# Softmax denominators taken off the output matmuls and summed elementwise, in a two-layer attention and convolution kernel

## The chip, the cores and the metric

One core of a Trainium2 chip (trn2). The metric is device time of one execution in microseconds; of several runs the median counts. Engines are named as in the profile: PE is TensorE (PEld its weight loads), DVE is VectorE, ACT ScalarE, POOL GpSimd, SP SyncE, which here only issues DMAs.

## What is computed

A backbone of two layers over 1024 latent tokens (width 1024) with a prefix of 256 context tokens, in float32. Layer 0 has two groups of heads: global attention over all 1280 tokens (A) and banded attention of 128-query blocks over the context and at most three neighbouring 128-key blocks (B), whose context queries also have a learned sink logit in the denominator. Layer 1 has a convolution branch and a 2-D neighbourhood attention with a bias table (D). Every attention is

```python
s = jnp.einsum("bqhgd,bkhd->bhgqk", q, k) * ATTN_SCALE + bias
p = jax.nn.softmax(s, axis=-1)
o = jnp.einsum("bhgqk,bkhd->bqhgd", p, v)
```

followed by a SiLU gate, an output projection, and a residual scaled by a modulation vector, `silu(c) @ mod_w + mod_b`. A last RMSNorm gives the result.

## The kernel before, in words

To keep float32 accuracy, matmul operands are split in two: `split` (L329) makes a high part on ACT (L331) and subtracts it from the source on POOL or DVE for the low part (L334). A product is then three matmuls, high·high, low·high and high·low; `mm3` (L352 to L354) does it for the projections.

**Attention** is one generator, `attn_gen` (L463), for both layers. Its work is a list of groups, and a group is a list of key tiles. In layer 0 a group is one 128-query block of one unit (`group0`, L621; four heads side by side, 512 columns). Units 2 and 3 are B, units 0 and 1 are A, in the order 2, 3, 0, 1. A B group has two context tiles and, for latent blocks (`qb >= 2`), two or three band tiles: 4 or 5 tiles, with 8 such groups in a unit. A context group has 2 tiles, and a latent A group 10. In layer 1 a group is one half of the grid of one head (`group1`, L1355): 7 tiles, of 512, 256, 352, 512, 320, 224 and 512 columns; there are 16 groups.

For a tile, PE forms the scores in bank `st` (L529, L533), ACT takes the exponential into `pf` (L541; in layer 1 DVE adds the bias first, L538), ACT makes `ph` and POOL, or every 12th (layer 0) or 5th (layer 1) time DVE, makes `pl`. Three tiles later `flush` (L470) adds the tile to the group's output bank `ov`, which has one buffer. The value tile is 192 wide: low part of V, high part of V, and 64 columns of ones. So three matmuls of the tile's columns,

```python
PE.matmul(o, V[:, 64:192], ph[:, :n], start=(t == 0), stop=False)
PE.matmul(g.ov[0:64, q0 : q0 + n], V[:, 0:64], ph[:, :n], start=False, stop=False)
PE.matmul(o, V[:, 64:192], pl[:, :n], start=False, stop=(last and g.sink is None))
```

(L480, L481, L482) give the output in rows 0 to 63 and the denominator, 64 times, in rows 64 to 127. After the last tile DVE transposes the denominators (L490), takes the reciprocal (L492), spreads it again (L493), and `finish` (L689 in layer 0, L1426 in layer 1) multiplies it onto the output (L693, L1430) and applies the gate (L695, L1432).

**Order.** `weave` (L562) advances the attention generator and a generator of other work by turns: in layer 0 the projections of the next unit, in layer 1 the projections `d_proj` of the last heads and the output projections `out1`. While units 2 and 3 are made, `tick` also advances `mod_steps` (L215), which computes eight 512-wide halves of the modulation vectors. For a half it loads two `mw` tiles of 1024 KB (L221) one half ahead, and multiplies each by four blocks of `csil` (`mod_part`, L181, matmuls at L185). Bank `tr` has one buffer too; layer 0 uses it for transposes of keys and queries (`trk`, L932). A scheduler then puts each engine's instructions in an order of its own, by priorities; on the chip every engine takes them strictly in that order, SP's DMA issues included.

Of the kernel before, what the change touches and what calls it, by code (L numbers as in the profile page):

```python
# [10 lines left out]
F32 = mybir.dt.float32  # L11
# [22 lines left out]
LOOK0, LOOK1 = 3, 3  # L34
AHEAD = 3
# [54 lines left out]
def tile_kernel(ctx: ExitStack, tc: tile.TileContext, a, out):  # L90
# [11 lines left out]
    mk, mwp, layer = [0], [None], [0]  # L102
# [112 lines left out]
    def mod_steps(pool, halves):  # L215

        def load(l, part, j):
            ws = []
            for d in (0, 4):
                w = pool.tile([P, 4, 512], F32, tag="mw", name=nm("mw"), bufs=2)  # L220
                SY.dma_start(w, mod_src(l, part, j, d, d + 4))  # L221
                ws.append(w)
            return ws

        ws = load(*halves[0])
        for n_, hf in enumerate(halves):
# [4 lines left out]
            for d, w in enumerate(ws):  # L231
                mod_part(pb, w, range(4 * d, 4 * d + 4))
# [5 lines left out]
            if n_ + 1 < len(halves):  # L238
                ws = load(*halves[n_ + 1])
# [156 lines left out]
    def v_tiles(pool, n, bufs=1):  # L396
        Vs[:] = [pool.tile([P, n, 192], F32R, tag="V", name=nm("Vt"), bufs=bufs) for _ in range(bufs)]
        for V in Vs:
            GP.memset(V[:, :, 128:192].bitcast(F32), 1.0)
# [63 lines left out]
    def attn_gen(pool, groups, vshare, look, nexts=None):  # L463
# [6 lines left out]
        def flush():  # L470
# [9 lines left out]
            PE.matmul(o, V[:, 64:192], ph[:, :n], start=(t == 0), stop=False)  # L480
            PE.matmul(g.ov[0:64, q0 : q0 + n], V[:, 0:64], ph[:, :n], start=False, stop=False)  # L481
            PE.matmul(o, V[:, 64:192], pl[:, :n], start=False, stop=(last and g.sink is None))  # L482
            if last:
                if g.sink is not None:
                    PE.matmul(g.ov, g.skm(), g.QL[0:76, :], start=False, stop=True)
                r1 = pool.tile([P, 8, 32], F32, tag="r1", name=nm("r1"), bufs=1)
                r8 = pool.tile([P, 8], F32, tag="r8", name=nm("r8"), bufs=2)
                rb = pool.tile([P, 256], F32, tag="rb", name=nm("rb"), bufs=1)
                for e in range(2):
                    VE.transpose(r1[e * 64 : (e + 1) * 64].rearrange("p a b -> p (a b)")  # L490
                                 .rearrange("p (a q) -> p a q", a=2), g.den(g.ov[64:128, :], e))
                VE.reciprocal(r8, r1[:, :, 0])  # L492
                VE.transpose(rb, r8[:, :, None].broadcast_to([P, 8, 32]))  # L493
                g.finish(g.ov, rb)
# [23 lines left out]
        for x, (g, t) in enumerate(items):  # L518
# [17 lines left out]
            pf = pool.tile([P, 512], F32, tag="pf" if layer[0] else "ost", name=nm("pf"), bufs=PFB)  # L536
# [7 lines left out]
            pend.append((g, t, ph, pl))  # L544
            if t == len(g.tiles) // 2:
                g.gate()
# [73 lines left out]

    def group0(u, qb):  # L621
# [64 lines left out]
        def den(dn, e):  # L686
            return dn.rearrange("p (e f q) -> p f e q", f=2, e=2)[:, :, e, :]

        def finish(ov, rb):  # L689
            y = a0.tile([P, 2, P], F32, tag="y", name=nm("y"), bufs=YB)  # L690
            for e in range(2):
                es = slice(e * 64, (e + 1) * 64)
                VE.tensor_tensor(y[es], den(ov[0:64, :], e), rb[es, :].rearrange("p (a q) -> p a q", a=2),  # L693
                                 op=ALU.mult)
# [4 lines left out]
            else:  # L699
# [7 lines left out]
                  tiles=[(k, 0, 512, x) for k, x in kt], den=den, finish=finish)  # L707
# [276 lines left out]
    with tc.tile_pool(name="o0", bufs=1, reuse_waits="tile") as op_:  # L984
# [49 lines left out]
        def final_proj(c):  # L1034
# [3 lines left out]
            pool, tag, bufs = (kvp, "QH", 3) if c == 2 else (op_, "acc1", 1)  # L1038
# [5 lines left out]
            for e in range(DK):  # L1044
# [15 lines left out]
                else:  # L1060
                    if c < 2:
                        sq = op_.tile([P, 512], F32, tag="sq1", name=nm("sq1"), bufs=3)
                    else:
                        sq = kvp.tile([P, 512], F32, tag="QL", name=nm("sq1"), bufs=3)
# [670 lines left out]
```

## Time and profile before

| | |
|---|---|
| three runs | 1527.92, 1532.71, 1538.26 us; median 1532.71 |
| the profiled execution | span 1528.5 us; the page gives no other time for it |
| busy share | PE 95%, PEld 76%, DVE 67%, POOL 52%, ACT 49% |
| layer 0's B units | about 120 to 500 us; A units to about 905 us |
| between the attentions | about 905 to 1170 us, projections and convolution |
| layer 1's attention | about 1200 to 1505 us |

Times in a trace count from the span's start. A row of a group gives line, engine, operation, tiles and shapes, how often it ran, its busy time and the mean of one in ns, and behind the bar the idle time of the engine just before. PE's busy time counts a matmul from start to modelled end, and neighbours overlap; what one costs in a stream is the distance from start to start.

### The profile page before, as it was taken

To read this page: it belongs to the slowest core of one execution; us is meant where nothing else is said; L and a number is where in the kernel's file an instruction comes from. 1 tells how busy PE (TensorE), PEld (TensorE's weight loads), DVE (VectorE), ACT (ScalarE), POOL (GpSimd) and SP (SyncE) were. 2 spreads that over 40 slices of the span, in tenths; PEclk is the share of its full clock that TensorE was granted. 3 is DMA by queue.
4 is the path that set the end of the run, shared out by engine and by line. 5 is a ranking of instruction groups with operands and counts; after the bars stand their busy time and mean duration, and the time that the engine had idled before them with its cause. 6 is when DMAs were issued, how large, how long until landed. Compare 5 with 4: busy or idle time off the path is not lost.

```text
span 1528.5 us, 21545 instructions
## 1 busy us (share of the span) xinstructions
PE 1451.0 (95%) x7144; PEld 1167.2 (76%) x7144; DVE 1031.7 (67%) x2095; ACT 748.1 (49%) x1418; POOL 788.0 (52%) x628
## 2 busy tenths in 40 slices
PE   6999999998998999999999889999999999989996
PEld 2786877896896777886777568888887788868775
DVE  2643566589578856457676948899848666567766
ACT  3642433443435564447646665343334455455564
POOL 3360443555454766557645665665532434364665
PEclk9999999999999999999999999999999999989998
DMA  9564325422312246121202021210484677877642
GB/s 366 201 225 135 106 69 174 135 77 88 114 56 76 85 138 210 49 69 54 59 28 66 35 67 56 62 56 28 158 253 144 207 219 240 248 222 234 178 129 110
DMA packets 154167, 199.83 MB, mean 131 GB/s; under 512 B 14716, under 2 KB 95816, under 8 KB 154056
## 3 DMA queue, kind: packets, MB, share of 16 engines
q1 hardware_dynamic: 147392, 186.88, 38.9%
q10 hardware_dynamic: 6664, 11.57, 2.3%
q8 instruction: 56, 0.92, 0.3%
q14 instruction: 55, 0.45, 0.1%
HBM read 148.07 MB, written 49.02 MB: 129 GB/s over the span
## 4 chain that ended last, share of the span: by engine, by line
PE 79%; DVE 11%; issue 3%; DMA 3%; ACT 2%; POOL 1%; ACTq 0%; SPq 0%; DVEq 0%; POOLq 0%
PE p L352 6%; PE p L354 6%; PE p L353 6%; PE ov L480 5%; PE ov L482 4%; PE ov L481 4%; PE po L352 4%; PE st L533 4%; PE st L529 4%; PE po L353 4%; PE po L354 4%; PE pq L352 4%; PE pq L353 3%; PE pq L354 3%; PE pg L352 2%
## 5 line engine op out<-in xcount | busy, mean ns | idle before, releaser
L334 POOL TENSOR_TENSOR pl<-pf,ph 128x512 fp32r<-128x512 f32 (+4 forms) x321 | 394.0, 1239 | 384.9 <-ACT ph L331 337.3
L541 ACT ACTIVATE pf<-st 128x512 f32<-128x512 f32 x284 | 166.5, 597 | 203.6 <-PE st L533 165.2
L334 POOL TENSOR_TENSOR wl<-wr,wh 128x512 fp32r<-128x512 f32 (+2 forms) x131 | 169.3, 1302 | 136.5 <-ACT wh L331 124.0
L331 ACT CAST ph<-pf 128x512 fp32r<-128x512 f32 (+4 forms) x364 | 209.5, 588 | 27.1 <-PE ov L481 15.9
L352 PE MATMUL p<-hh,wh 128*128 128x512 f32 x448 | 176.0, 393 | 3.4 <-DVE spq L1233 1.3
L353 PE MATMUL p<-hl,wh 128*128 128x512 f32 x448 | 174.5, 390 | 0.0
L354 PE MATMUL p<-hh,wl 128*128 128x512 f32 x448 | 173.0, 391 | 0.0
L480 PE MATMUL ov<-ph,Vt 128*128 128x512 f32 (+4 forms) x364 | 141.0, 387 | 4.2 <-DVE y L693 2.0
L529 PE MATMUL st<-QH,KAt 128*128 128x512 f32 (+4 forms) x364 | 140.2, 386 | 3.9 <-ACT pf L541 3.1
L482 PE MATMUL ov<-pl,Vt 128*128 128x512 f32 (+4 forms) x364 | 141.1, 388 | 2.2 <-POOL pl L334 2.1
L481 PE MATMUL ov<-ph,Vt 128*64 128x512 f32 (+4 forms) x364 | 138.9, 381 | 0.0
L533 PE MATMUL st<-QL,KBt 68*128 68x512 f32 (+4 forms) x364 | 136.4, 386 | 0.9 <-issue 0.8
L1177 DVE SCALAR_TENSOR_TENSOR cps<-U,taps,cps 128x512 f32<-128x512 f32 x184 | 125.9, 748 | 0.7
L331 ACT CAST wh<-wr 128x512 fp32r<-128x512 f32 (+2 forms) x134 | 80.9, 613 | 84.1 <-PE po L353 15.9
L352 PEld LDWEIGHTS p<-hh,wh 128*128 128x128 f32 x448 | 84.2, 188 | 21.5 <-ACT spq L1231 1.6
L656 DVE TENSOR_REDUCE mp<-mx 128x1 f32<-128x512 f32 x128 | 85.3, 681 | 19.3 <-PE mx L655 18.3
L354 PEld LDWEIGHTS p<-hh,wl 128*128 128x128 f32 x448 | 84.1, 188 | 17.4
L353 PEld LDWEIGHTS p<-hl,wh 128*128 128x128 f32 x448 | 84.2, 188 | 17.1 <-issue 0.2
L1020 DVE SCALAR_TENSOR_TENSOR x<-po,modT,x 128x512 f32<-128x512 f32 (+1 forms) x72 | 46.9, 657 | 64.0 <-PE po L354 63.5
L352 PE MATMUL pq<-wh,hh 128*128 128x384 f32 x256 | 88.2, 344 | 1.0 <-ACT hh L331 1.0
L353 PE MATMUL pq<-wl,hh 128*128 128x384 f32 x256 | 87.3, 341 | 0.0
L354 PE MATMUL pq<-wh,hl 128*128 128x384 f32 x256 | 86.6, 342 | 0.0
(287 smaller groups left out, 3417.2 us busy)
## 6 DMA issues: line engine op xcount, KB each, us to landing
mw<-in_mod_w_dram SPq DMA_DIRECT2D x16, 1024.0 KB, 5.3
Q<-qs SPq DMA_DIRECT2D x40, 256.0 KB, 2.1
QH<-Q SPq DMA_DIRECT2D x80, 128.0 KB, 2.7
mw<-in_mod_w_dram SPq DMA_DIRECT2D x16, 512.0 KB, 6.8
wr<-in_od_d_dram SPq DMA_DIRECT2D x32, 256.0 KB, 3.1
wr<-in_ev_qkv_dram SPq DMA_DIRECT2D x16, 384.0 KB, 5.0
KAt<-KD SPq DMA_DIRECT2D x16, 384.0 KB, 6.5
wr<-in_od_wo_dram SPq DMA_DIRECT2D x22, 256.0 KB, 3.4
```

What stands on the lines that cost most here:

```text
L331: acts.append(SC.copy(hi, src))
L334: (GP if leng == "g" else VE).tensor_tensor(lo, src, hi.bitcast(F32), op=ALU.subtract)
L352: PE.matmul(o, lh, rh, start=first, stop=False)
L353: PE.matmul(o, lh, rl, start=False, stop=False)
L354: last.append(PE.matmul(o, ll, rh, start=False, stop=end))
L480: PE.matmul(o, V[:, 64:192], ph[:, :n], start=(t == 0), stop=False)
L481: PE.matmul(g.ov[0:64, q0 : q0 + n], V[:, 0:64], ph[:, :n], start=False, stop=False)
L482: PE.matmul(o, V[:, 64:192], pl[:, :n], start=False, stop=(last and g.sink is None))
L529: sts.append(PE.matmul(st[:, :n], KA[:, cs], g.QH[:, q0 : q0 + n], start=True, stop=False))
L533: PE.matmul(st[:, :n], KB[0:68, cs], g.QL[0:68, q0 : q0 + n], start=False, stop=True)
L541: acts.append(SC.activation(pf[:, :n], st[:, :n], AF.Exp, scale=1.0 if g.bias else SCALE))
L1177: VE.scalar_tensor_tensor(pc, uc, w, pc, op0=ALU.mult, op1=ALU.add)
```

## The change

Where a group has `adds` set (latent groups of units 2 and 3, 16 in all, and all 16 groups of layer 1), the ones no longer go through the matmul of every tile:

- the exponentials of the group's first tile are written to an accumulator `acc`, and each later tile's `pf` is added to it, on POOL or, for every fourth tile (`t = 4` in layer 0, `t = 2` and `t = 6` in layer 1), on DVE;
- per tile PE does two matmuls instead of three: both halves of V by `ph` at once, with the low part of V into rows 0 to 63 of `ov` and the high part into rows 64 to 127, and the high part by `pl` into rows 0 to 63. The low·high product therefore waits in the other half of the bank;
- at the end of the group `acc` is split into two parts (ACT and DVE) and multiplied by 64 columns of ones, two matmuls of 512 columns into a bank `dn` of tag `tr`, and the sink follows;
- `finish` first copies rows 64 to 127 of `ov` to SBUF on ACT and adds rows 0 to 63 on DVE, which frees `ov`, and then transposes, inverts and multiplies. In layer 1 both transposes run over 64 x 512 instead of 64 x 256 twice and 128 x 256.

Other groups do as before. `mod_steps` loads tiles of 512 KB, three buffers instead of two of 1024 KB, and issues the load of chunk n+3 after the matmuls of chunk n. Layer 1's value tile is 128 wide, and its fill with ones is gone. Between the layers some scratch tiles change their pool.

```diff
+ADV = (0, 2)
+UADD = (2, 3)
...
-        ws = load(*halves[0])
+        ws = []
+        for n in range(3):
+            load(n)
...
-            for d, w in enumerate(ws):
-                mod_part(pb, w, range(4 * d, 4 * d + 4))
+            for d in range(4):
+                mod_part(pb, ws.pop(0), (2 * d, 2 * d + 1))
+                if 4 * n_ + d + 3 < 4 * len(halves):
+                    load(4 * n_ + d + 3)
...
-            PE.matmul(o, V[:, 64:192], ph[:, :n], start=(t == 0), stop=False)
-            PE.matmul(g.ov[0:64, q0 : q0 + n], V[:, 0:64], ph[:, :n], start=False, stop=False)
-            PE.matmul(o, V[:, 64:192], pl[:, :n], start=False, stop=(last and g.sink is None))
-            if last:
+            if g.adds:
+                both = [(o, V[:, 0:128], ph), (o[0:64], V[:, 64:128], pl)]
+                for x_, v_, p_ in both[::-1] if last else both:
+                    PE.matmul(x_, v_, p_[:, :n], start=(t == 0 and p_ is ph), stop=(last and p_ is ph))
...
+            if g.adds:
+                dn = bank("tr", nm("dn"))
+                for k_, x in enumerate(g.acs):
+                    PE.matmul(dn[0:64, :], ones64[0] if layer[0] else V[:, 128:192], x, start=(k_ == 0), stop=(k_ == 1 and g.sink is None))
...
+            if g.adds and t == 0:
+                pf = g.acc = pool.tile([P, 512], F32, tag="acc", name=nm("acc"), bufs=2)
...
+            if g.adds and t > 0:
+                a_ = g.acc[:, q0 : q0 + n]
+                (VE if (t + ADV[layer[0]]) % 4 == 0 else GP).tensor_tensor(a_, a_, pf[:, :n], op=ALU.add)
+            if g.adds and t == len(g.tiles) - 1:
+                g.acs = [pool.tile([P, 512], F32R, tag=x, name=nm("ac" + x), bufs=look + 1) for x in ("ph", "pl")]
+                split(g.acc, *g.acs, "s", "v")
...
+    def ADDS(u, qb):
+        return qb >= 2 and u in UADD
...
+                acts.append(SC.copy(y[ds], ov[64:128, :]))
+                VE.tensor_tensor(y[ds], ov[0:64, :], y[ds], op=ALU.add)
+                VE.transpose(r1[ds].rearrange("p a b -> p (a b)"), dn[0:64, :])
+                VE.reciprocal(r8[ds], r1[ds, :, 0])
+                rb = dlow.tile([P, 512], F32, tag="r1", name=nm("rb"), bufs=1)
+                VE.transpose(rb[ds], r8[ds, :, None].broadcast_to([64, 16, 32]))
+                VE.tensor_tensor(y[ds], y[ds], rb[ds], op=ALU.mult)
```

How the scheduler places it, at three places. First PE at the end of layer 1's last group (`ov` the output, `trs` the column sums of the last norm). Before:

```order
L480 MATMUL ov_15325<-ph_15360,Vt_11676 128x320
L481 MATMUL ov_15325<-ph_15360,Vt_11676 64x320
L482 MATMUL ov_15325<-pl_15361,Vt_11676 128x320
L480 MATMUL ov_15325<-ph_15414,Vt_11676 128x224
L481 MATMUL ov_15325<-ph_15414,Vt_11676 64x224
L267 MATMUL trs_15571<-ones,sq_3731_15355 128x2
L482 MATMUL ov_15325<-pl_15415,Vt_11676 128x224
L480 MATMUL ov_15325<-ph_15467,Vt_11676 128x512
L481 MATMUL ov_15325<-ph_15467,Vt_11676 64x512
L267 MATMUL trs_15571<-ones,sq_3737_15384 128x2
```

Here `trs` fills the wait for the last `pl`. With the change:

```order
L483 MATMUL ov_15594<-ph_15628,Vt_11854 128x320
L483 MATMUL ov_15594<-pl_15629,Vt_11854 64x320
L483 MATMUL ov_15594<-ph_15682,Vt_11854 128x224
L483 MATMUL ov_15594<-pl_15683,Vt_11854 64x224
L483 MATMUL ov_15594<-pl_15736,Vt_11854 64x512
L483 MATMUL ov_15594<-ph_15735,Vt_11854 128x512
L493 MATMUL dn_15823<-acph_15742,one_11839 64x512
L493 MATMUL dn_15823<-acpl_15743,one_11839 64x512
L269 MATMUL trs_15843<-ones,sq_3840_15623 128x2
```

Two rows a tile instead of three, and `trs` now stands behind both `dn`.

Second, PE at the seventh half of the modulation (`pm` its bank, `mw` its weights), in the B units. Before, eight blocks from two tiles that were loaded a half earlier:

```order
L185 MATMUL pm_3143<-mw_2212,csil 32x512 x4
L185 MATMUL pm_3143<-mw_2214,csil 32x512
L353 MATMUL pq_3092<-wl_3075,hc_171 128x384
L354 MATMUL pq_3092<-wh_3074,hc_171 128x384
L352 MATMUL pq_3092<-wh_3074,hc_171 128x384
```

With the change:

```order
L187 MATMUL pm_3248<-mw_2076,csil 32x512 x2
L187 MATMUL pm_3248<-mw_2080,csil 32x512 x2
L187 MATMUL pm_3248<-mw_2084,csil 32x512 x2
L535 MATMUL st_3270<-QH_2902,KAt_489 128x512
L681 MATMUL mx_2950<-KAt_489,QH_2902 128x384
L483 MATMUL ov_3267<-pl_3006,Vt_490 64x512
L483 MATMUL ov_3267<-ph_3024,Vt_490 128x512
L483 MATMUL ov_3267<-pl_3025,Vt_490 64x512
L483 MATMUL ov_3267<-ph_3141,Vt_490 128x512
L187 MATMUL pm_3248<-mw_3251,csil 32x512 x2
```

The fourth chunk (`mw_3251`) is loaded into the buffer that the first one (`mw_2076`) leaves, so its DMA starts only after the first row here, and eight other matmul rows stand between.

Third, DVE in layer 1 at the end of a group (`yo` the output). Before:

```order
L490 STREAM_TRANSPOSE r_3468_14450<-ov_14289 64x256 x2
L538 TENSOR_TENSOR pf_14442<-st_14437,bs_14348 128x352
L436 TENSOR_REDUCE nmt_14313<-mp_14252 128x4
L492 RECIPROCAL r_3469_14451<-r_3468_14450 128x8
L493 STREAM_TRANSPOSE rb_14452<-r_3469_14451 128x256
L538 TENSOR_TENSOR pf_14477<-st_14472,bs_14368 128x512
L1430 TENSOR_TENSOR yo<-ov_14289,rb_14452 64x256 x2
```

With the change:

```order
L1463 STREAM_TRANSPOSE r_3625_14902<-dn_14899 64x512
L1462 TENSOR_TENSOR yo<-ov_14729,yo 64x512
L1535 SCALAR_TENSOR_TENSOR x_3329_13914<-po_3683_15083,modT_103,xs_15079 128x256
L1535 SCALAR_TENSOR_TENSOR x_3331_13916<-po_3683_15083,modT_103,xs_15079 128x256
L1464 RECIPROCAL r_3626_14903<-r_3625_14902 64x16
L547 TENSOR_TENSOR pf_14968<-st_14963,bs_14840 128x320
L1447 ISA mx_3614_14863,mp_14853<-mx_3614_14863,bm_14823 128x440
```

`ov` is now read by one DVE row early on, and the wider reciprocal chain follows without it.

More of the change, by code (lines that the diff above doesn't have):

```diff
@@ L101, in tile_kernel @@
     turn = [0, 0]
-    mk, mwp, layer = [0], [None], [0]
+    mk, mwp, layer, ones64 = [0], [None], [0], []
     sts = []
@@ L215, in mod_steps, with load @@
     def mod_steps(pool, halves):
[L217 to L223, printed above, removed]
-        ws = load(*halves[0])
+        def load(n):
+            l, part, j = halves[n // 4]
+            w = pool.tile([P, 2, 512], F32, tag="mw", name=nm("mw"), bufs=3)
+            SY.dma_start(w, mod_src(l, part, j, 2 * (n % 4), 2 * (n % 4) + 2))
+            ws.append(w)
+        ws = []
+        for n in range(3):
+            load(n)
         for n_, hf in enumerate(halves):
@@ L396, in v_tiles @@
     def v_tiles(pool, n, bufs=1):
[L397 to L399 removed]
+        Vs[:] = [pool.tile([P, n, P], F32R, tag="V", name=nm("Vt"), bufs=bufs) for _ in range(bufs)]
     def k_tiles(pool, hi, n, bufs=1):
@@ L479, in flush @@
             o = g.ov[:, q0 : q0 + n]
-            PE.matmul(o, V[:, 64:192], ph[:, :n], start=(t == 0), stop=False)
-            PE.matmul(g.ov[0:64, q0 : q0 + n], V[:, 0:64], ph[:, :n], start=False, stop=False)
-            PE.matmul(o, V[:, 64:192], pl[:, :n], start=False, stop=(last and g.sink is None))
-            if last:
-                if g.sink is not None:
[L485 to L494, printed above, removed]
+            if g.adds:
+                both = [(o, V[:, 0:128], ph), (o[0:64], V[:, 64:128], pl)]
+                for x_, v_, p_ in both[::-1] if last else both:
+                    PE.matmul(x_, v_, p_[:, :n], start=(t == 0 and p_ is ph), stop=(last and p_ is ph))
+            else:
+                PE.matmul(o, V[:, 64:192], ph[:, :n], start=(t == 0), stop=False)
+                PE.matmul(o[0:64], V[:, 0:64], ph[:, :n], start=False, stop=False)
+                PE.matmul(o, V[:, 64:192], pl[:, :n], start=False, stop=(last and g.sink is None))
+            if not last:
+                return
+            if g.adds:
+                dn = bank("tr", nm("dn"))
+                for k_, x in enumerate(g.acs):
+                    PE.matmul(dn[0:64, :], ones64[0] if layer[0] else V[:, 128:192], x, start=(k_ == 0), stop=(k_ == 1 and g.sink is None))
+                if g.sink is not None:
+                    PE.matmul(dn[0:64, :], g.skm()[:, 64:128], g.QL[0:76, :], start=False, stop=True)
+                g.finish(g.ov, dn)
+                return
+            if g.sink is not None:
+                PE.matmul(g.ov, g.skm(), g.QL[0:76, :], start=False, stop=True)
+            g.finish(g.ov, g.ov[64:128, :])
         if layer[0]:
@@ L706, in group0 @@
                   sink=(sink[:, hs : hs + 4], sink8[:, hs : hs + 4]) if isb else None, skm=lambda: sk, k=lambda: (KAs[u], KBs[u]),
-                  tiles=[(k, 0, 512, x) for k, x in kt], den=den, finish=finish)
+                  tiles=[(k, 0, 512, x) for k, x in kt], finish=finish, adds=ADDS(u, qb))
         g.prep = attn_prep(kvp, g)
```

58 lines of the change are left out of this document (35 added, 23 removed).

## The prediction

> **What bounds the kernel now.** I read the page first (busy shares, then the chain of work that ended last), then the busy time of each engine by stage, then PE's timeline. The page:
>
> ```profile
> span 1528.5 us, 21545 instructions
> PE 1451.0 (95%) x7144; PEld 1167.2 (76%) x7144; DVE 1031.7 (67%) x2095; ACT 748.1 (49%) x1418; POOL 788.0 (52%) x628
> PE 79%; DVE 11%; issue 3%; DMA 3%; ACT 2%; POOL 1%; ACTq 0%; SPq 0%; DVEq 0%; POOLq 0%
> ```
>
> PE is busy 95% of the span and is 79% of the chain. Shares of the span hide stages, so the next view is busy time by stretch: after the stretch come its length, then PE, PEld, DVE, ACT and POOL, then the granted clock and DMA. The stretches are the B units, two halves of layer 1's attention with eight groups each, and the end.
>
> ```profile
> 120.00:500.00 380.00, 369.11 (x1901) 306.77 (x1901) 254.75 (x609) 153.99 (x330) 168.35 (x126) 0.99 0.32 102
> 1200.00:1360.00 160.00, 154.18 (x795) 129.01 (x796) 102.03 (x245) 88.07 (x176) 74.70 (x68) 0.97 0.80 236
> 1360.00:1500.00 140.00, 136.35 (x664) 111.33 (x663) 100.68 (x220) 80.66 (x154) 82.70 (x74) 1.00 0.59 169
> 1500.00:1528.50 28.50, 17.04 (x118) 14.03 (x117) 18.55 (x51) 9.78 (x24) 12.49 (x13) 0.74 0.40 148
> ```
>
> In the three stretches that the change touches PE idles 10.9, 5.8 and 3.7 us; the rest is matmul behind matmul. So a matmul less is time less there, until another engine's results come late. The nearest such engine is DVE, with 67%, 64% and 72%.
>
> **PE: what a matmul costs.** Busy time overstates it, so I take distances from start to start. PE's timeline near the end of layer 1 (start, duration, line, tiles, shape):
>
> ```profile
> 1489.61 0.39 PE L480 MATMUL ov<-ph,Vt 128*128 128x512 f32 x1
> 1489.84 0.39 PE L481 MATMUL ov<-ph,Vt 128*64 128x512 f32 x1
> 1490.06 0.40 PE L482 MATMUL ov<-pl,Vt 128*128 128x512 f32 x1
> 1490.30 0.28 PE L480 MATMUL ov<-ph,Vt 128*128 128x256 f32 x1
> 1490.41 0.28 PE L481 MATMUL ov<-ph,Vt 128*64 128x256 f32 x1
> 1490.65 0.33 PE L480 MATMUL ov<-ph,Vt 128*128 128x352 f32 x1
> 1490.81 0.32 PE L481 MATMUL ov<-ph,Vt 128*64 128x352 f32 x1
> 1498.00 0.31 PE L480 MATMUL ov<-ph,Vt 128*128 128x320 f32 x1
> 1498.15 0.31 PE L481 MATMUL ov<-ph,Vt 128*64 128x320 f32 x1
> 1498.45 0.27 PE L480 MATMUL ov<-ph,Vt 128*128 128x224 f32 x1
> 1498.55 0.27 PE L481 MATMUL ov<-ph,Vt 128*64 128x224 f32 x1
> ```
>
> A matmul of 512 columns shows 0.39 us but the next starts 0.23 us later; 352 columns take 0.16, 320 take 0.15, 256 take 0.11 and 224 take 0.10. A weight block of 64 columns instead of 128 changes nothing.
>
> *Layer 1.* Each of 16 groups loses one matmul per tile: three of 512 columns (0.69), one each of 256, 352, 320 and 224 (0.52), 1.21 us; it gains two of 512 for `dn`, 0.46. Net 0.75, times 16: **-12.0 us**. *B units.* The 16 groups have 76 tiles (six of 5 and two of 4 tiles in a unit, two units), so 76 matmuls go and 32 come: 44 times 0.23, **-10.1 us**. Together **-22.1 us**.
>
> [...]
>
> **DVE and POOL: what takes over the work.** Groups by form, layer 1 from 1200 to 1500 us (count, busy us, mean ns, then idle before):
>
> ```profile
> L538 DVE TENSOR_TENSOR pf<-st,bs 128x512 f32<-128x512 f32 x16 | 10.8, 673 | 0.3 <-PE ov L481 0.2
> L490 DVE STREAM_TRANSPOSE r<-ov 64x256 f32<-64x256 f32 x30 | 13.6, 452 | 4.5 <-PE ov L482 3.9
> L493 DVE STREAM_TRANSPOSE rb<-r 128x256 f32<-128x256 f32 x15 | 6.6, 441 | 0.3
> L1430 DVE TENSOR_TENSOR yo<-ov,rb 64x256 f32<-64x256 f32 x24 | 10.0, 415 | 0.5
> L1432 DVE SCALAR_TENSOR_TENSOR yo<-yo,gt 64x512 f32<-64x512 f32 x12 | 11.1, 924 | 0.3
> L334 DVE TENSOR_TENSOR pl<-pf,ph 128x512 fp32r<-128x512 f32 x9 | 6.3, 698 | 1.7 <-ACT ph L331 1.4
> L334 DVE TENSOR_TENSOR pl<-pf,ph 128x352 fp32r<-128x352 f32 x3 | 1.5, 492 | 0.0
> L334 POOL TENSOR_TENSOR pl<-pf,ph 128x512 fp32r<-128x512 f32 x39 | 51.4, 1321 | 68.9 <-ACT ph L331 63.7 <-PE ov L482 3.4 <-PE po L354 1.6
> L334 POOL TENSOR_TENSOR pl<-pf,ph 128x320 fp32r<-128x320 f32 x12 | 10.7, 894 | 16.0 <-PE ov L482 7.5 <-ACT ph L331 6.2 <-PE st L533 2.3
> L334 POOL TENSOR_TENSOR pl<-pf,ph 128x256 fp32r<-128x256 f32 x13 | 9.6, 738 | 15.5 <-ACT ph L331 12.3 <-PE po L354 1.8 <-PE mx L1413 1.3
> ```
>
> *Layer 1, DVE per group.* Gone: two transposes (0.90), one (0.44), two products (0.83), 2.17 us. New: the sum of the two halves of `ov` (64 x 512 out of PSUM, as L538: 0.67), two transposes of 64 x 512 (not in the trace; 0.45 for 256 columns, with the 1 ns per column of the other rows an estimate of 0.71 each; bounds 0.45 and 0.90), a product 64 x 512 in SBUF (0.69 to 0.92 by L334 and L1432; 0.8), two additions to `acc` (352 and 512 columns, 0.49 and 0.70) and the low part of `acc` (0.70): 4.78 us. The reciprocal stays. Net +2.6, plus 0.2 because SBUF-only rows stretch: +2.8 a group, 22 us in each half of layer 1. DVE then has 124 of the 154 us left of the first half (81%) and 123 of the 134 of the second (92%).
>
> *B units, DVE per group:* the low part of `acc` (0.70), an addition in 12 of 16 groups (0.53 on average), one product more in `finish` (some 0.5 between L1430's 0.42 and L334's 0.70): 1.7 us, 28 in all, 283 of 370 (76%).
>
> *POOL:* per layer-1 group additions of 256, 512, 320 and 224 columns, 0.74 + 1.32 + 0.89 + some 0.7, 3.6 us or 58 in all: 215 of 288 us (75%). B: 48 additions at 1.32, 63 us, 232 of 370 (63%). *ACT* gains the high part of `acc` and one or two copies, about 1.3 us a group, and stays below 70%. None of these engines is full on average, so their work is hidden, except where DVE's queue is.
>
> What a full DVE costs PE, I read in stretches of 20 us of the same attention:
>
> ```profile
> 340.00:360.00 20.00, 17.82 (x100) 13.55 (x99) 18.53 (x33) 7.62 (x16) 13.11 (x11) 1.00 0.37 114
> 440.00:460.00 20.00, 20.00 (x112) 18.59 (x111) 16.43 (x41) 6.00 (x12) 9.83 (x8) 1.00 0.23 67
> 460.00:480.00 20.00, 16.74 (x71) 12.49 (x69) 17.50 (x45) 9.72 (x18) 10.08 (x8) 0.91 0.11 34
> 500.00:520.00 20.00, 17.41 (x109) 15.14 (x107) 19.15 (x32) 10.14 (x24) 12.92 (x10) 1.00 0.32 102
> 1440.00:1460.00 20.00, 20.00 (x100) 16.75 (x99) 16.14 (x34) 11.95 (x23) 13.30 (x13) 1.00 0.62 183
> ```
>
> With DVE at 16.1 and 16.4 of 20 us PE stays full; at 17.5 to 19.2 it loses 2.2 to 3.3. About ten stretches newly come above 17: the second half of layer 1 (134 us, 6.7 of them) and some three late in the B units. Bounds 0 and 2.2 each, 0 to +22 us. I take a third, **+7**, since rows on both sides of the line are close.
>
> [...]
>
> ```profile
> L490 DVE STREAM_TRANSPOSE r<-ov x112: 451/453/455, 163.3 to 1502.2; 64x256 f32<-64x256 f32 x112
> L1432 DVE SCALAR_TENSOR_TENSOR yo<-yo,gt x12: 670/689/1579, 1221.7 to 1433.0; 64x512 f32<-64x512 f32 x12
> ```
>
> The transpose out of PSUM never varies, the SBUF-only row goes from 670 to 1579 ns. All additions that move to POOL and DVE are SBUF-only. This stands behind the rival in which DVE becomes the bound.
>
> **The modulation chunks.** Loads before, 1024 KB in the B units and 512 KB at the start:
>
> ```profile
> mw<-in_mod_w_dram SPq DMA_DIRECT2D x16, 1024.0 KB, 5.3
> mw<-in_mod_w_dram SPq DMA_DIRECT2D x16, 512.0 KB, 6.8
> ```
>
> The fourth chunk of a half is loaded after the first one's matmuls. In the seventh half the order puts about 2.2 us of PE work between (two more chunks and six rows, estimated with the distances above); in the fourth 1.4, in the fifth 3.2, in the eighth 3.5, elsewhere 4.7 or more. Against a landing of 5.3 us PE would wait 3.1, 3.9, 2.1 and 1.8, 11 in all; half the bytes should land sooner, and SP issues the load behind other stores, which delays it. In the gap PE also waits for DVE's maxima, which lengthens it. Behind the waiting matmul stands all of PE's attention. Bounds 0 and +11, I take **+3**.
>
> **The end.** After the last tile the path is addition, split, `dn` (0.46), then a second transpose wider by some 0.27, and `trs` starts only behind `dn`; `ov` itself is freed earlier. Bounds 0 and +2, I take **+1**. `dn` also holds the single `tr` bank, which the key transposes of layer 0 wait for; the order already places them behind it, and I cost it at nothing, covered by projection matmuls (without them 16 times the 0.45 of a transpose, +7, in the range). Layer 1's fill with ones and the pools between the layers: nothing, ahead of or beside full PE stretches.
>
> Sum: -22.1 + 7 + 3 + 1 = **-11.1**. The profiled execution would go from 1528.5 to 1517.4. It is 4.2 us below the median of 1532.71, so the median would be **1521.6 us**.
>
> **Rivals.** *The whole saving arrives.* DVE's work falls in holes, as in the two rows with 16 us and full PE, and the chunks come in time: -22.1 + 1, **1511.6**. For it: PE idles only 2 to 4% today. Against it: 92% in the second half of layer 1.
>
> *DVE becomes the bound* (the other side). Place: groups 9 to 16 of layer 1 and the B units from 300 us on, where five stretches are already over 17. In-order DVE rows come late, `pf` and the maxima with them, and PE stands. Price: 2.2 us for each of 6.7 + 8 stretches, 32, and 3 + 1 as above: -22.1 + 36, **1547**. It beats the saving from 1.2 us a stretch on. For it: the three rows with PE at 17; against it: the fullest DVE stretches here also hold phase ends.
>
> *The chunk loads decide.* The full 11 us at the chunks, 7 for the `tr` bank, 1 at the end and 2 for DVE: -22.1 + 21, **1531.6**, no change. The matmuls are gone, but PE waits at the chunks or for `dn` instead. For it: the landing of 5.3 us against gaps of 1.4 to 3.5. Against it: only four of eight halves have such gaps.
>
> **How the numbers follow.** Chances: forecast 0.50, whole saving 0.28, chunk loads 0.12, DVE bound 0.10. A measurement of this kernel tells about 1% (15 us) from no change. Faster by over 1% (below 1517.4) takes most of the whole-saving case and a quarter of the forecast's: 0.37. Slower by over 1% takes the upper half of the DVE case and a little more: 0.07. Within: 0.56. Range: down to 1505, where also `ov`'s earlier release pays (all idle time before L480 is some 4 us) and the whole saving; up to 1541, short of the DVE case's middle.
>
> **What would show it.** Right: about 188 output matmuls fewer and 64 on `dn`; layer 1's stretch from its first to its last output some 6 us shorter, the B units' some 5; DVE near 90% in the last 130 us of layer 1. PE waiting for `pf`, maxima or `dn` through DVE there would show the +7; waits of L187 for `mw` in the B units the +3. Wrong: PE idle as small as before in all stretches (then the whole saving arrives), or DVE's SBUF-only rows at 1.2 us and more with PE below 18 of 20 us through layer 1 (then DVE is the bound).

## The result and the profile after

The changed kernel takes **1590.83 us** (median of four runs, 1589.35 to 1592.6) against 1532.86 for the kernel before in the same comparison: a ratio of **1.0379, interval 1.0354 to 1.0404**, 58 us slower. The prediction said 1521.6 and a range of 1505 to 1541: wrong in sign and in size. The page of the changed kernel, with the chain that ended last as its third line:

```profile
span 1588.5 us, 21681 instructions
PE 1462.2 (92%) x7020; PEld 1164.0 (73%) x7020; DVE 1143.9 (72%) x2172; ACT 786.2 (49%) x1498; POOL 926.0 (58%) x738
PE 4%; DVE 2%; POOL 1%; ACT 1%; issue 0%; DMA 0%; DVEq 0%; SPq 0%; POOLq 0%; ACTq 0%
```

The matmuls are gone as announced: 7144 - 188 + 64 = 7020. But PE is busy longer, with 124 matmuls fewer, and its share fell from 95% to 92%; DVE gained 112 us and POOL 138. The chain of the third line was followed only for some 8% of the span here, so I read stages instead. Busy time by engine in the stretches that answer to those of the prediction (shifted so that each begins and ends at about the same work):

```profile
120.00:517.00 397.00, 359.88 (x1756) 289.72 (x1756) 289.06 (x628) 172.89 (x366) 224.46 (x168) 0.92 0.31 97
1245.00:1406.00 161.00, 150.45 (x759) 123.44 (x759) 129.58 (x265) 94.68 (x192) 110.78 (x101) 0.95 0.80 236
1406.00:1551.00 145.00, 135.32 (x606) 106.00 (x607) 126.15 (x230) 85.74 (x165) 116.06 (x102) 0.95 0.57 161
1551.00:1588.50 37.50, 22.09 (x130) 17.19 (x128) 23.54 (x54) 13.24 (x30) 16.29 (x16) 0.69 0.31 113
```

The four stretches grew by 17, 1, 5 and 9 us; PE's idle time in them went from 10.9, 5.8, 3.7 and 11.5 us to 37.1, 10.5, 9.7 and 15.4. The cut between the two halves of layer 1 hides something. Counted from the first output matmul of a group, the first eight groups took 159.5 us before and 154.4 now, the other eight 138.7 and 150.0. So the first half did gain 5 of its forecast 6 us; the second, where DVE is busy for 131 of the 150 us, lost 11, which is 17 short of its saving.

The column behind the engines is new as a cause: the granted clock fell from 0.99, 0.97, 1.00 and 0.74 to 0.92, 0.95, 0.95 and 0.69. Length times the missing share of the clock was 16 us before and is 59 now. Part of that falls into PE's idle time, so 43 us more is an upper bound; but the low clock also holds behind the waits: from 362 to 366 us PE was busy for all of the 4 us at a granted clock of 0.50, and matmuls of 512 columns started 0.43 us after one another (L483 at 363.30 and 363.73), where the prediction's rows have 0.23. The rest of the 60 us between the profiles lies where the change adds no work. Before, the A units (500 to 900) and the stretch between the layers:

```profile
500.00:900.00 400.00, 381.22 (x1745) 291.88 (x1743) 262.87 (x464) 237.22 (x419) 252.78 (x190) 0.98 0.24 76
900.00:1200.00 300.00, 290.19 (x1364) 241.23 (x1363) 238.65 (x397) 124.13 (x205) 145.76 (x113) 0.98 0.36 114
```

After:

```profile
517.00:934.00 417.00, 397.95 (x1850) 310.62 (x1849) 277.43 (x493) 240.54 (x431) 260.14 (x196) 0.98 0.23 75
934.00:1245.00 311.00, 293.45 (x1366) 242.92 (x1364) 242.55 (x398) 125.06 (x206) 147.10 (x111) 0.98 0.35 110
```

The A units take 17 us more because 105 more matmuls run there: projections that filled PE in the B units before and now come later. So the B units cost 17 us in their own stretch and 17 that they push on. Between the layers 11 us more go by with the same work.

**Where PE stands.** The heart of the loss is the first half of unit 3:

```profile
330.00:350.00 20.00, 14.30 (x56) 7.70 (x55) 18.63 (x38) 8.88 (x17) 16.61 (x12) 0.91 0.50 157
350.00:370.00 20.00, 11.72 (x33) 7.67 (x33) 19.91 (x38) 7.29 (x16) 13.14 (x10) 0.58 0.11 32
370.00:390.00 20.00, 16.89 (x67) 13.74 (x68) 17.28 (x42) 9.53 (x23) 13.20 (x11) 0.74 0.17 55
390.00:410.00 20.00, 14.84 (x65) 11.70 (x64) 18.96 (x41) 8.56 (x20) 12.89 (x11) 0.77 0.45 138
```

DVE is at 17 to 20 of 20 us, PE at 12 to 17 and a granted clock of 0.58 to 0.91. Between 350 and 370 PE runs 33 matmuls where the prediction's full stretches had 100 to 112. DVE's timeline there (start, duration, line, tiles):

```profile
354.23 1.01 DVE L721 TENSOR_TENSOR y<-y,rb 128x256 f32<-128x256 f32 x1
355.17 1.23 DVE L254 SCALAR_TENSOR_TENSOR nr<-nt,nr 128x10 f32<-128x10 f32 x1
...
357.66 0.82 DVE L941 TENSOR_TENSOR pc<-pc,gain 128x640 f32<-128x640 f32 x1
358.40 0.15 DVE L446 TENSOR_TENSOR nmt<-se,nmt 128x4 fp32r<-128x4 f32 x1
358.52 0.49 DVE L950 TENSOR_TENSOR rt<-pc,k_cs 128x320 f32<-128x320 f32 x1
358.93 1.75 DVE L556 TENSOR_TENSOR acc<-acc,pf 128x512 f32<-128x512 f32 x1
```

And PE's in the same stretch, with its wait in brackets:

```profile
358.61 0.38 PE L457 MATMUL trn<-ident,nmt 128*12 128x128 f32 x1 [2.91 <-DVE nmt L446]
...
361.39 0.69 PE L493 MATMUL dn<-acph,Vt 128*64 128x512 f32 x1 [1.91 <-ACT acph L333]
```

The product of the finish (L721, 1.01 us) and ten elements a partition (L254, 1.23 us) stand ahead of the short `nmt` for which PE waits 2.91 us. Then the last addition takes 1.75 us, `acph` follows it, and PE waits 1.91 us more before `dn`. That `dn` of 512 columns shows 0.69 us at a granted clock of 0.50, where such a matmul showed 0.39 before at 1.00.

The order also leaves PE nothing else here. In the fifteen tiles from the first of unit 3 on (321.3 to 377.3 us) PE runs 3 us of projections and key transposes, with some 70 us of them still to come; in the kernel before it ran 31 us in the same fifteen tiles (columns of `pq`, `pg` and `trk` in the traces, at the 0.23 us for 512 of the prediction).

### The profile page after: what moved, and what is told of

Read it like the earlier page. It is cut to its first block, busy times and chain, and to the rows that moved or that the text cites. A ratio compares the mean times of both kernels' runs of the same rounds, so it can differ in the third digit from the quotient of the medians.

```text
span 1588.5 us, 21681 instructions
## 1 busy us (share of the span) xinstructions
PE 1462.2 (92%) x7020; PEld 1164.0 (73%) x7020; DVE 1143.9 (72%) x2172; ACT 786.2 (49%) x1498; POOL 926.0 (58%) x738
## 5 line engine op out<-in xcount | busy, mean ns | idle before, releaser
L336 POOL TENSOR_TENSOR pl<-pf,ph 128x512 fp32r<-128x512 f32 (+4 forms) x292 | 365.4, 1260 | 174.0 <-ACT ph L333 116.4
L550 ACT ACTIVATE pf<-st 128x512 f32<-128x512 f32 x252 | 149.2, 596 | 141.0 <-PE st L539 85.8
L333 ACT CAST ph<-pf 128x512 fp32r<-128x512 f32 (+1 forms) x332 | 192.1, 584 | 29.7 <-PE dn L493 7.7
L535 PE MATMUL st<-QH,KAt 128*128 128x512 f32 (+4 forms) x364 | 146.5, 404 | 12.4 <-ACT pf L550 7.4
L556 POOL TENSOR_TENSOR acc<-acc,pf 128x512 f32<-128x512 f32 (+2 forms) x112 | 127.9, 1142 | 34.5 <-ACT pf L548 25.1
L539 PE MATMUL st<-QL,KBt 68*128 68x512 f32 (+4 forms) x364 | 140.1, 396 | 0.8 <-issue 0.8
L535 PEld LDWEIGHTS st<-QH,KAt 128*128 128x128 f32 x364 | 71.6, 197 | 38.7 <-ACT pf L550 13.1
L336 POOL TENSOR_TENSOR pl<-acc,ph 128x512 fp32r<-128x512 f32 x29 | 40.2, 1387 | 82.7 <-PE st L535 35.6
```

What stands on the lines that cost most here:

```text
L333: acts.append(SC.copy(hi, src))
L336: (GP if leng == "g" else VE).tensor_tensor(lo, src, hi.bitcast(F32), op=ALU.subtract)
L535: sts.append(PE.matmul(st[:, :n], KA[:, cs], g.QH[:, q0 : q0 + n], start=True, stop=False))
L539: PE.matmul(st[:, :n], KB[0:68, cs], g.QL[0:68, q0 : q0 + n], start=False, stop=True)
L550: acts.append(SC.activation(pf[:, :n], st[:, :n], AF.Exp, scale=1.0 if g.bias else SCALE))
L556: (VE if (t + ADV[layer[0]]) % 4 == 0 else GP).tensor_tensor(a_, a_, pf[:, :n], op=ALU.add)
```

## The experiments

All ratios are against the kernel before, run beside each kernel; a per cent is 15.3 us. Line numbers are those of each kernel. My first theory was that the group ends cost the time: split, products on the ones and longer finish come late on a full DVE, and PE has nothing else to do. Its first rivals were the modulation's chunks and a full DVE in layer 1.

**Which part of the change.** Four kernels: additions in layer 0 only (layer 1 as before), in layer 1 only (`UADD = ()`), the new `mod_steps` alone in the kernel before, and that with the moved scratch tiles:

```diff
-            pool, tag, bufs = (kvp, "QH", 3) if c == 2 else (op_, "acc1", 1)
+            pool, tag, bufs = (kvp, "QH", 3) if c == 2 else (a0, "acc", 2)
...
-                        sq = op_.tile([P, 512], F32, tag="sq1", name=nm("sq1"), bufs=3)
+                        sq = op_.tile([P, 512], F32, tag="sq1", name=nm("sq1"), bufs=2)
```

> This kernel has the additions in units 2 and 3 of layer 0 only, the smaller modulation chunks and the moved scratch tiles; layer 1's attention is as before. The changed kernel is 58 us slower than the one before, and its stages show unit 3 and the filling work that it pushes into the A units some 43 us longer, the stretch between the layers 12, layer 1's attention about even and the end 9. Theory 1, group ends: at the end of a B group the sum's split, the products on the ones and the longer finish come late on a full DVE, PE stands and the scheduler has no projection work there: nearly all of the loss is in this kernel, +40 to +55 us. Theory 2, modulation chunks: +40 to +55 as well, but then the kernel with the chunks alone shows it too. Theory 3, DVE full in layer 1, where its share is highest: 0 to +15 here.

> The additions in layer 1 only; units 2 and 3 of layer 0 go by three matmuls a tile as before; the smaller modulation chunks and the moved scratch tiles stay. Theory 1, group ends in the B units: +5 to +20 us, made of the longer end (9), the stretch between the layers (up to 12) and layer 1's attention about even. Theory 2, modulation chunks: +45 to +60, since the B units lose as much as in the full change. Theory 3, DVE full in layer 1: +30 or more, with PE idle through the second half of layer 1.

> The kernel before with the smaller modulation chunks alone; no additions, no scratch tile moved. Theory 1, group ends: -3 to +5 us, the chunks cost no more than the 3 us of the prediction. Theory 2, modulation chunks: +25 us or more, with PE waiting at the modulation's matmuls for their DMA. Theory 3: as theory 1.

> The kernel before with the smaller modulation chunks and the scratch tiles between the layers in the other pool, with one buffer fewer for the squares; no additions anywhere. If the scratch tiles make the stretch between the layers longer, as the changed kernel's stages have it, this is +8 to +14 us over the kernel with the chunks alone; if what is late there comes from the additions, it is within 3 us of it. Theory 2 has +25 us or more for the chunks in it, theories 1 and 3 have nearly nothing.

Measured: layer 0 only **1.0275** (1.0251 to 1.0299), layer 1 only **1.0146** (1.0114 to 1.0178), chunks **1.0004** (0.9986 to 1.0023), chunks and scratch tiles **1.0060** (1.0040 to 1.0080). The chunks are free, which ends theory 2. The scratch tiles cost 0.56%, 8.6 us, at the lower edge of the 8 to 14 expected for what they do between the layers. The profiled executions are 4.5 us apart, all of it between the layers. What POOL waited for there, with chunks and scratch tiles:

```profile
POOL acc L1067 <- DMA X<-x: 13.6, 1, 13.6
```

and with the chunks alone, where that row is missing and POOL's first sum waits only for its squares:

```profile
POOL acc L1067 <- ACT sq L1065: 4.9, 2, 2.6
```

Above that base layer 0 adds 2.15% and layer 1 0.86%; with the base they sum to 3.6%, near the 3.8% of the whole change. So both layers lose, though both do less on PE. Theory 3 (layer 1 as the only place) falls, though the 11 us of its second half are real; theory 1 has the place right in layer 0, and in layer 1 lie 22 us against its 5 to 20.

**What the end of the program costs.** PE behind the last tile with chunks and scratch tiles:

```profile
1510.20 1.62 PE L267 MATMUL trs<-ones,sq 128*128 128x2 f32 x14
1511.67 0.47 PE L482 MATMUL ov<-pl,Vt 128*128 128x512 f32 x1
1515.00 1.23 PE L278 MATMUL bc<-ident,nr 128*128 128x128 f32 x4 [2.85 <-DVE nr L252]
```

With the additions in layer 1, PE, then DVE, then ACT:

```profile
1523.34 0.44 PE L493 MATMUL dn<-acpl,one 128*64 128x512 f32 x1
1525.57 3.77 PE L269 MATMUL trs<-ones,sq 128*128 128x2 f32 x16 [1.79 <-DVE r L1463]
1530.97 1.22 PE L354 MATMUL po<-od,wh 128*128 128x256 f32 x4 [1.62 <-ACT od L333]
```

```profile
1527.20 0.69 DVE L1467 TENSOR_TENSOR y<-y,rb 64x512 f32<-64x512 f32 x1
1529.38 0.16 DVE L272 TENSOR_SCALAR rbv<-trs 128x4 f32<-128x4 f32 x1 [1.49 <-PE trs L269]
1529.58 0.69 DVE L1468 SCALAR_TENSOR_TENSOR y<-y,gt 64x512 f32<-64x512 f32 x1
```

```profile
1530.30 0.61 ACT L333 CAST od<-y 64x512 fp32r<-64x512 f32 x1 [5.22 <-DVE y L1468]
```

Before, 14 `trs` ran in the wait for the last `pl`, 0.12 us each at a granted clock of 1.00. Now all 16 come after `dn`, at 0.50, 0.24 us each. DVE's order puts `rbv`, which needs them, ahead of the gate (L1468), which was ready at 1527.9; the gate waits 1.5 us, and the last projection with it.

**Which work inside it.** All additions on DVE; all on POOL; none; and `dn` in the maxima's banks:

```diff
-                (VE if (t + ADV[layer[0]]) % 4 == 0 else GP).tensor_tensor(a_, a_, pf[:, :n], op=ALU.add)
+                VE.tensor_tensor(a_, a_, pf[:, :n], op=ALU.add)
...
-                dn = bank("tr", nm("dn"))
+                dn = bank("mx", nm("dn"))
```

> The changed kernel with every addition to acc on DVE, none on POOL. The changed kernel takes 1590.8 us. Theory A, DVE is the bound at the group ends (19.4 to 19.8 of 20 us in unit 3): POOL's 112 additions become some 60 us more for DVE, and the time rises to 1600 to 1630. Theory B, POOL's additions are the cost (its queue makes the low parts late, and DVE's SBUF-only rows stretch beside them): 1560 to 1580, and DVE's rows of 128x10 elements fall from some 900 ns towards 700. Theory C, the length of the chain behind a group's last tile, whichever engine adds: 1585 to 1597.

> The changed kernel with every addition to acc on POOL, none on DVE. Theory A, DVE is the bound: DVE loses 44 additions, some 30 us of work, and the time falls to 1570 to 1582. Theory B, POOL's additions are the cost: 1597 to 1615. Theory C, the chain's length: 1587 to 1600, a little longer because POOL's addition takes 1.3 us instead of 0.7.

> The changed kernel with all additions to acc left out, and the first tile's exponential taken of zero, so that the denominators are constants; the split of acc, the products on the ones and the finish stay. It prices the additions against the rest of the group's end. Theory A, DVE is the bound: 30 us less DVE work, 1570 to 1582, like the kernel with all additions on POOL. Theory B, POOL's additions are the cost: 1540 to 1555. Theory C, the chain of split, products and finish: 1580 to 1590, since only the last addition's latency goes.

> The changed kernel with the denominators' bank dn in the two banks of the maxima instead of the single bank tr. The prediction gave tr no cost, up to 7 us. Theory D, the single bank: dn waits for the modulation's and the keys' use of tr and they for dn, and the end of the program waits for it: 15 us or more come back, 1575 or less. Theories A, B and C: 1585 to 1597, the bank only changes places.

Measured: all on DVE **1.0525** (1.0486 to 1.0564), 1615.8 us; all on POOL **1.0475** (1.0433 to 1.0516), 1607.0; no additions **1.0140** (1.0107 to 1.0172), 1556.2; `dn` in the other banks **1.0362** (1.0327 to 1.0398), 1590.0. Theory D falls: nothing near 15 us comes back. In this kernel the order also puts 30 us of projections into the first fifteen tiles of unit 3, and layer 0 takes 813 us from its first score to its last output against 816 in the changed kernel. So the projections missing there are not the cause by themselves. A foresaw the DVE kernel and missed the POOL kernel, B the reverse: either engine makes it worse, and the split between them is the best of the three. Without additions 2.4%, 37 us, come back, a microsecond short of what B foresaw: they are the largest item. C, the chain's length, missed all three. But 1.4% stay, although this kernel has the full saving on PE.

The 22 us of that rest were divided by leaving out the split as well:

```diff
-                g.acs = [pool.tile([P, 512], F32R, tag=x, name=nm("ac" + x), bufs=look + 1) for x in ("ph", "pl")]
-                split(g.acc, *g.acs, "s", "v")
+                g.acs = [ph, pl]
```

> The changed kernel with the additions left out and also the split of acc: the products on the ones take the last tile's own two parts, with the last tile's exponential taken of zero like the first one's, so the denominators are constants. The two products, the copy of ov and the longer finish stay. It divides the 22 us that the kernel without additions still loses. If the split (0.6 us on ACT, 1.0 on DVE, and two of the four buffers of ph and pl held until the products) is what the group's end costs: 1530 to 1542, 14 us or more under the kernel without additions. If the copy and the longer finish on DVE cost it: 1548 to 1556.

Measured **1.0203** (1.0178 to 1.0228), 1564.3 us: with less work 8 us slower than with the split. Neither expectation holds, and the comparison says nothing of the split before the scatter of such edits is known (below).

**Do the additions need a chain to be dear?** The old three matmuls, and additions whose sum nobody reads:

> The kernel before with the smaller chunks and the moved scratch tiles (0.6% over before), and the 60 additions to acc of units 2 and 3 beside the old three matmuls a tile: the sums are formed and not used, so nothing waits for them but the buffers of the exponentials, and no split, no product on the ones and no longer finish follows. Theory B, the additions' time on POOL and DVE is a cost by itself: +1.4 to +2.2% over before, as much as the changed kernel lost by its additions in layer 0 (14 us between the changed kernel and the one without additions). Theory C, only the chain behind the last addition makes them costly: within 4 us of the kernel with chunks and scratch tiles alone, +0.4 to +0.9%.

Measured **1.0213** (1.0189 to 1.0238), 1.5% over its base. So theory C is not needed for them: 60 additions whose sum nobody reads cost about 23 us. By stage, the profiled execution is 14 us longer in the B units, where the additions run, and 9 in the A units and 3 between the layers, where none run and the work is the same. So 14 us lie where the additions are, as many as the profiled layer 0 loses when they are left out of the changed kernel; the other 12 may be the order's. What they occupy was then told apart, by adding the accumulator to itself, on the same engines and on DVE alone:

```diff
-                (VE if (t + ADV[layer[0]]) % 4 == 0 else GP).tensor_tensor(a_, a_, pf[:, :n], op=ALU.add)
+                (VE if (t + ADV[layer[0]]) % 4 == 0 else GP).tensor_tensor(a_, a_, a_, op=ALU.add)
```

> The kernel with the unused additions of units 2 and 3 (+2.1% over before, +1.5% over the same kernel without them), but each of the 60 additions takes the accumulator twice instead of the new exponentials: same engines, same size, same places, and no buffer of the exponentials is held for it. The order alone scatters by up to 0.8%. If the time of POOL and DVE themselves is the price: +1.7 to +2.6%. If the price is that the exponentials' two buffers come free only after the addition, so that the exponentials two tiles on are late: +0.4 to +1.2%.

> The same with all 60 of these additions on DVE, none on POOL, and no buffer of the exponentials held. DVE gets some 48 rows of about 0.8 us more, POOL 48 of 1.3 us fewer. If DVE's time is what PE waits for: +2.2 to +3.2%, more than with 12 of them on DVE. If POOL's queue is the price: +0.6 to +1.4%, less than with 48 of them on POOL. If only the held buffers are: +0.4 to +1.2% in both of these kernels.

Measured **1.0168** (1.0131 to 1.0206) and **1.0206** (1.0179 to 1.0233). The first is just under what the engines' own time would give (1.7 to 2.6) and over all that the held buffers would (0.4 to 1.2); the second lies between its two ranges, nearer to the one for DVE. POOL's row is also cheaper here (1133 ns with one source, 1338 with two), so the buffers' share, the 0.45% between the first and the unused additions, is an upper bound and within the scatter. The additions in the three kernels, unused, then idle source, then on DVE:

```profile
L552 POOL TENSOR_TENSOR acc<-acc,pf 128x512 f32<-128x512 f32 x48 | 64.2, 1338 | 11.2 <-ACT pf L546 9.3 <-PE trk L940 0.9 <-PE pq L354 0.5
L552 DVE TENSOR_TENSOR acc<-acc,pf 128x512 f32<-128x512 f32 x12 | 10.9, 911 | 2.9 <-ACT pf L546 2.5 <-POOL acc L552 0.4
```

```profile
L552 POOL TENSOR_TENSOR acc<-acc 128x512 f32<-128x512 f32 x48 | 54.4, 1133 | 1.1
```

```profile
L552 DVE TENSOR_TENSOR acc<-acc 128x512 f32<-128x512 f32 x60 | 63.9, 1065 | 2.2 <-POOL pl L336 1.5
```

**Where in layer 0.** Additions in unit 2 alone and in unit 3 alone (`UADD = (2,)`, `(3,)`):

> The additions in unit 2 only; unit 3 and layer 1 as before, smaller chunks and moved scratch tiles kept (0.6% over before without any addition). Theory of the cover: in unit 2 DVE has room (13.4 us of 20 on average up to 300 us) and projections fill PE, so the 5 us of removed matmuls arrive: 1534 to 1542, +0.1 to +0.6%. Theory of the chain: every group loses the same, half of the 35 us that both units lose beyond chunks and scratch tiles: +1.5 to +2.0%.

> The additions in unit 3 only, else as the kernel with unit 2 alone. Theory of the cover: DVE is already at 17 to 19 of 20 us here and the waits come one behind the other with TensorE at half clock, so nearly the whole loss of both units is here: 1568 to 1578, +2.3 to +2.9%. Theory of the chain: +1.5 to +2.0%, like unit 2 alone.

Measured **1.0167** (1.0145 to 1.0189) and **1.0208** (1.0188 to 1.0228). Above their base these are 1.1 and 1.5%: unit 2 loses as the theory of the chain has it, unit 3 a little more, and the theory of the cover falls. But unit 2's loss shows at another place. Without additions, early in unit 3:

```profile
340.00:360.00 20.00, 19.84 (x114) 18.02 (x112) 17.50 (x35) 9.69 (x22) 13.20 (x10) 1.00 0.19 64
400.00:420.00 20.00, 20.00 (x102) 16.58 (x101) 12.76 (x29) 7.85 (x18) 5.44 (x5) 0.96 0.33 112
```

With additions in unit 2 alone:

```profile
340.00:360.00 20.00, 14.56 (x55) 8.94 (x54) 19.77 (x47) 10.66 (x21) 13.26 (x9) 0.91 0.29 85
400.00:420.00 20.00, 13.76 (x62) 8.52 (x60) 18.32 (x41) 13.33 (x29) 12.42 (x9) 0.99 0.34 108
```

Unit 3's own attention is unchanged there, yet PE's matmuls fall to about half: few projections run beside it. When the 37th tile of the B units starts (298.6 us against 282.9 without additions), PE has done 157 us of projections and transposes against 141, counted as above. So unit 2 had lost nothing by then; its 16 us more went into projections, and in the first twelve tiles of unit 3 (323.7 to 358.8 us) only 3 us of them run. That they were used up early is not enough as a reason, though. The kernel before had done 155 us by its 37th tile, at 301.0 us, and its order still ran 29 us of them in the first twelve tiles of unit 3. Where an order places the fill is what differs; no run tells how much of that the additions force.

**Work, or a new order?** Any edit makes the scheduler order the whole program anew, so an order may be lost that happened to lie well. A shift of the count that gives every 12th and 5th low part to DVE keeps the work and changes the order:

```diff
-            split(pf[:, :n], ph[:, :n], pl[:, :n], "s", "v" if cnt[0] % vshare == 0 else "g")
+            split(pf[:, :n], ph[:, :n], pl[:, :n], "s", "v" if (cnt[0] + 4) % vshare == 0 else "g")
```

> The kernel before, with the tiles whose low part DVE makes shifted by four in the count (still every 12th in layer 0 and every 5th in layer 1): the same work on each engine, give or take one tile, but the scheduler's order differs from there on. Theory W, the added work and its chain are what costs: within 8 us of before, -0.5 to +0.5%. Theory O, the loss comes from losing an order in which the fill happens to lie well, which any edit of the program disturbs: +0.8 to +2.0% here too.

> The kernel before with the same shift by eight instead of four; a second draw of the order with the same work. Theory W: -0.5 to +0.5%. Theory O: +0.8 to +2.0%.

> The changed kernel with the same shift by four. Theory W: +3.3 to +4.3%, as the changed kernel (+3.8%) with half a per cent of scatter. Theory O: a new draw of the order, anywhere from +1.5 to +4.5%, and the mean of the changed draws lies no more than 1% above the mean of the shifted kernels before.

> The changed kernel with the shift by eight. Theory W: +3.3 to +4.3%. Theory O: +1.5 to +4.5%, differing by more than 1% from the one with the shift by four.

Measured: before with the shifts **1.0020** (1.0001 to 1.0039) and **1.0081** (1.0054 to 1.0108), the changed kernel with them **1.0401** (1.0372 to 1.0431) and **1.0429** (1.0402 to 1.0456). Three orders of the old work lie at 0, 0.2 and 0.8%, three of the new at 3.8, 4.0 and 4.3%. Theory O wanted the means of the two within 1% of each other; they lie 3.6% apart, and theory W's ranges hold but for one shift of the old kernel, 0.3% outside. The gap is the work's; the order scatters by up to 0.8%, 12 us. The three new orders are alike in one thing, the 1 to 3 us of projections in the first twelve tiles of unit 3; the kernel with `dn` in the maxima's banks is not, and lies at 3.6%. The scatter is also the doubt on each single comparison above: the split's 0.6%, the buffers' 0.45% and the scratch tiles' 0.56% lie inside it (the last has the wait for `X` in its trace for it), units 2 and 3 and layer 1, at 1.1, 1.5 and 0.9%, not far outside, the 2.4% of the additions well outside.

## Why the prediction was wrong, by its own steps

- **PE, -22.1: the count was right, and the spacing held.** In the changed kernel, rows of 512, 256 and 352 columns start 0.24, 0.11 and 0.16 us after one another:

```profile
1500.65 0.40 PE L483 MATMUL ov<-ph,Vt 128*128 128x512 f32 x1
1500.89 0.39 PE L483 MATMUL ov<-pl,Vt 128*64 128x512 f32 x1
1501.12 0.28 PE L483 MATMUL ov<-ph,Vt 128*128 128x256 f32 x1
1501.23 0.28 PE L483 MATMUL ov<-pl,Vt 128*64 128x256 f32 x1
1501.35 0.32 PE L483 MATMUL ov<-ph,Vt 128*128 128x352 f32 x1
```

- **"None of these engines is full on average, so their work is hidden": the step that failed.** The loads themselves were forecast well. DVE was put at 283, 124 and 123 us in the B units and the halves of layer 1 and has 289, 130 and 126; POOL was put at 232 and 215 us in the two attentions and has 224 and 227. As shares of the longer stretches that is only 73, 80 and 87% of DVE, 57 and 74% of POOL: neither is full on average, and yet the work was not hidden. Unused additions, mostly on POOL, cost 14 us in the B units alone; all additions cost 37. PE takes the results in its order, three tiles ahead, so a late one stops it before another engine is full on average (2.91 us for `nmt` and 1.91 for `acph` in the stretch above), unless a projection lies ready. In the changed B units 16 of PE's 36 us of waiting are for DVE's maxima and shifts (`mp`, `nmt`) and hardly any for low parts; in layer 1 POOL's low parts lead, 4.2 us, before DVE's sum with the bias, 3.8.
- **DVE full, +7 (0 to 22): mis-sized.** Additions on DVE were put at 0.49 and 0.70 us, the low part of `acc` at 0.70; in layer 1 they took:

```profile
L556 DVE TENSOR_TENSOR acc<-acc,pf 128x512 f32<-128x512 f32 x15 | 14.4, 961 | 5.9 <-ACT pf L550 3.4 <-ACT ph L333 1.9 <-POOL pl L336 0.4
L556 DVE TENSOR_TENSOR acc<-acc,pf 128x352 f32<-128x352 f32 x16 | 13.1, 821 | 3.2 <-POOL acc L556 2.3 <-POOL wl L336 0.8
L336 DVE TENSOR_TENSOR acpl<-acc,acph 128x512 fp32r<-128x512 f32 x15 | 12.6, 843 | 1.4 <-ACT acph L333 1.4
```

  These are 0.14 to 0.33 us over their prices; the 0.2 us a group for rows that stretch was my estimate, which no row gives. More than that, a stretch with a full DVE was priced by rows of before, 2.2 us of PE, and 2.2 is the smallest of the three rows shown, which lose 2.2, 3.3 and 2.6. The four stretches of unit 3 shown above lose 22 us of 80, 5.6 each, at a granted clock of 0.58 to 0.91. The second half of layer 1, where 6.7 stretches or 15 us were the upper bound of the loss, came out 17 us short of its saving. That the price of before held only while projections stood ready is argued from unit 3, not tested.
- **The chunks, +3: held within its bounds.** 0.0% (-0.1 to +0.2) alone, with PE waiting for `mw` twice in the changed B units, 2.8 us. A load of 512 KB there landed 4.9 us after its issue in the median (L222, 3.6 to 7.2), one of 1024 KB before 5.3.
- **`tr` at nothing: held** (1.0362 with `dn` elsewhere, 1.0379 with it there). **The pools between the layers at nothing: wrong**, by 4.5 us (profiles) to 8.6 (ratios); the trace shows POOL waiting there for the DMA of `X`, 13.6 us.
- **The end, +1: wrong.** The last stretch grew by 9 us, 8 of them behind the last output matmul. The chain was added up at full clock and without DVE's order: `trs` doubled from 0.12 us each at a granted clock of 1.00 to 0.24 at 0.50, and the gate came behind `rbv`.
- **The rivals.** "DVE becomes the bound" had the right side and the right places, the B units from 300 us on and groups 9 to 16 of layer 1, at 1547 and a chance of 0.10. It named one engine where two count: with all additions on POOL, off DVE, the time rose too. "The whole saving arrives" spoke from PE's small idle time; that idle time was small while projections filled it, which says nothing of room on DVE and POOL.

In sum, with the ratios above: scratch tiles +9, additions +37, and the removed matmuls, split, products, finish and end together +12, which is 34 more than the -22 of the matmuls. The profiled executions tell where. The additions' share, 34 us between them, is 14 in layer 0, 15 in layer 1's attention and 5 at the end. Without additions, against the same kernel with chunks and scratch tiles alone, layer 0 is 17 us longer, the stretch between the layers 5, the end 4, and layer 1's attention 9 us shorter. So in layer 1 most of the forecast 12 us arrive once the additions are gone. What stays open is layer 0, +17 where -10 was forecast: no run divides it between split, products, finish and the order. Separate buffers for the two parts of `acc`, which now hold two of the four buffers of `ph` and `pl` (ACT's `ph` rows wait 7.7 us for `dn`), were not tried; nor were unused additions in layer 1. None of the eighteen kernels is faster than the one before.

## What to carry to other kernels

A full PE with small waits says that its cover is sufficient for the work as it is, not that the engines beside it have room: before moving work to them, put in dummy rows of that size, whose result nobody reads, and time them. Price PE's waits with the granted clock measured behind them (0.50 from 362 to 366 us here), and look at where the new order places the work that filled PE before. An edit that lets a scheduler order the program anew needs a second and third order of the same work before a per cent is believed.

## What the runs showed of the hardware

- **The clock was low behind a wait, not only in it.** In the kernel with additions in layer 1, PE was busy for 3.13, 1.85 and 3.70 of 4 us in these stretches, at a granted clock of 1.00, 0.75 and 0.50:

```profile
1518.00:1522.00 4.00, 3.13 (x14) 2.20 (x12) 1.75 (x3) 2.48 (x5) 4.00 (x5) 1.00 0.00 0
1522.00:1526.00 4.00, 1.85 (x6) 0.97 (x6) 3.06 (x5) 1.51 (x3) 2.42 (x2) 0.75 0.00 0
1525.50:1529.50 4.00, 3.70 (x16) 3.56 (x16) 2.41 (x5) 0.00 (x0) 0.00 (x0) 0.50 0.00 0
```

  From 1520.3 us to the `trs` PE waited 0.29, 0.94 and 1.79 us; the last of these waits, shown above, ended at 1525.57, and the 16 `trs` behind it ran at 0.50. What lowers the clock was not shown: no run varied the waits alone.
- **With additions on POOL, DVE's other rows took longer.** With the 60 unused additions DVE's total rose from 1037.2 to 1067.5 us, 30.3, of which the 12 on DVE are 10.9: the other 19 us are rows that were there before, beside 64 us of additions on POOL. In the idle-source kernel the same sum leaves 19 us beside 54. Of the rows out of PSUM, `r<-ov` of 64x256 kept its time (452 and 453 ns); of the short rows that lie in SBUF alone, `nmt<-se,nmt` went from 267 to 484 ns on average. The size, some 0.3 us of DVE for each us of such work on POOL, is an estimate from these profiles and rough: with all 60 on DVE its total rose by 54.1, 10 us less than the 63.9 that they took, so its other rows differ by that much too.
